# The first weight pair by eight plain products, x loaded in the order of need, and another machine model behind the instruction order

## The chip, the cores and the metric

The kernel runs on one core of a Trainium2 chip. The metric is the device time of one execution in microseconds (us); lower is better. A core has five engines that run side by side, each working through its own list of instructions in order: PE multiplies matrices, DVE (VectorE), ACT (ScalarE) and POOL (GpSimd) work element by element, and SP issues transfers between the chip's memory (HBM) and the core's own memory. POOL and ACT issue some transfers too. PE writes into eight banks of its own, each of 128 rows by 512 numbers.

## The reference

The reference is an encoder of two layers on x of 512 positions and 1024 channels. Cut to what matters:

```python
for l in range(2):
    h = rmsnorm(x, ffn1_norm[l]);  x = x + 0.5 * ((silu(h @ w_gate) * (h @ w_up)) @ w_down)
    h = rmsnorm(x, mix_norm[l]);   x = x + concat(pool, fourier, attention of h @ w_in) @ w_out
    h = rmsnorm(x, ffn2_norm[l]);  x = x + 0.5 * ((silu(h @ w_gate) * (h @ w_up)) @ w_down)
return rmsnorm(x, final_norm)
```

There are four such feed-forward blocks (1024 to 2816 and back) and two mixers. All is float32. The change touches the start of the first feed-forward block, and the order of instructions everywhere.

## The kernel before

**Layout.** x is held transposed as eight tiles `X[k]` of 128 channels by 512 positions. To keep float32 accuracy, every operand of a matmul is split into a rounded part and the remainder (`split`, L102 to L104: ACT writes `hi`, DVE writes `lo`), and one product is three matmuls: hi by hi, lo by hi, hi by lo.

**A feed-forward block.** `ffn` (L431) runs over 11 pairs of hidden row tiles in three chunks of 4, 4 and 3 pairs. After each chunk comes its part of `w_down` (tiles `dn`, 512 columns wide, L107 to L109). One pair is a `Unit` (L372). Its weights are four blocks of 512 KB, a11, a12, a21, a22: the first digit is the row tile, the second says whether they multiply the even or the odd tiles of x. The positions are halved too (`TH` = 256), so that a pair is a 2 by 2 by 2 block product. It is done with seven products in place of eight, by sums of weight blocks and sums of x blocks. One product (`product`, L378) is 24 matmuls of 256 columns, lines L386 to L388.

**Sums of weights.** A block goes by SP to one of seven staging tiles `st` (`load`, L154 to L161). A second block is added onto it in the staging tile by a transfer that POOL issues: on loading (L160, for a21 + a22) or after the tile has been split (L175, `then`). The next operand that uses the tile waits for that transfer. Splits are made three operands ahead of the one in use (`AHEAD`), into four `hi` and four `lo` tiles. `load` runs five blocks ahead (`RAWS`).

**Sums of x.** `PairNorm.scaled` (L293) multiplies each tile by its gain (tile `xg`, L296), and for each pair of tiles makes four sums of half tiles (`ta`, `tb`, L302 to L305) and four splits (`xo`, `xh`, `xl`): seven operands, by number 1 to 7.

**A unit's order.** `head` makes products 5 (sum a21 + a22) and 1 (a11); the tail of the unit before makes 4 and 3; `middle` makes 6, 7 and 2. The rms factor is applied late: `nm.end()` in the first unit's middle sums the squares across channels with two matmuls into a bank `ss` and computes the factor on DVE (L229 to L249). The squares are made by ACT (L274) and added up by POOL (L278; the last by DVE).

**The start.** SP loads the constants, then x (L194), with the first two weight blocks between. The first unit has its head `swapped`: product 1 of a11 comes first. Five matmuls on zeros (L212) run while nothing has arrived.

**What sets the order.** The code is traced in program order. On leaving the `TileContext`, the builder orders each engine's instructions: it plays the program on a model of the machine and lets each engine take the instruction that is ready in that model and stands first in the program. Buffers and banks are given out in the same pass. On the chip each engine then keeps to that list. Within the mixers the program order is the list `ORDER`, and `ON_VECTOR` and `ON_SCALAR` say which engine makes certain steps.

Of the kernel before, what the change touches and what calls it, by code (L numbers as in the profile page):

```python
# [66 lines left out]
def build(tc, xt, gu, dn, qk, wv, wfa, wo, pw, fw, small, lamv, alibi, dft_c, dft_s, out):  # L67
# [3 lines left out]
    with (  # L71
# [50 lines left out]
        for l in range(L):  # L122
            for n in range(2):
                i = 2 * l + n
                if n:
                    src = {f"P{h}": qk[l, h] for h in range(NH)}
                    src |= {"V0": wv[l, 0], "V1": wv[l, 1], "A": wfa[l, 1], "F": wfa[l, 0]}
                    src |= {"W0a": wo[l, 0], "W1a": wo[l, 1], "W2": wo[l, 2], "W3": wo[l, 3]}
                    for x in ORDER:
                        if x in src:  # L130
                            for z in range(2):
                                operand_of(raw(src[x][:, z * 1024 : (z + 1) * 1024]), eng=V if x in ON_VECTOR else G)
                for c0, c1 in CHUNKS:
                    tail = []
                    for u in range(c0, c1):
                        a11, a21, a22, a12 = [gu[i, u][:, q * 1024 : (q + 1) * 1024] for q in range(4)]
                        if raws:
                            t, t11 = raw(a21, plus=a22), raw(a11)
                        else:
                            t11, t = raw(a11), raw(a21, plus=a22)  # L140
                        t12, t22 = raw(a12), raw(a22)
                        head = [(t, a11), (t11, a21)]
                        for x, then in (head if recipes else head[::-1]) + tail + [(t, a12), (t11, None), (t12, None)]:
                            operand_of(x, then=then)
                        tail = [(t22, None), (t, None)]
                    for x, then in tail:
                        operand_of(x, then=then)
                    for m in range(KT):
                        w = 2 * (c1 - c0) * P
                        operand_of(raw(dn[i, m][:, 2 * c0 * P : 2 * c1 * P], w), w)  # L150
# [39 lines left out]
        sm = cp.tile([P, NSMALL], F32, name="sm")  # L190
        nc.sync.dma_start(sm, small)
        X = [cp.tile([P, S], F32, name=f"x{k}") for k in range(KT)]
        for k in range(KT):
            nc.sync.dma_start(X[k], xt[k])  # L194
            if k % 2:
                load(min(k // 2 + 1, 2 + (k > 6)))
        al = cp.tile([P, 896], F32, name="al")
        ident = cp.tile([P, P], F32, name="ident")
        make_identity(nc, ident)
# [58 lines left out]
        class Norm:  # L258
# [10 lines left out]
                V.tensor_scalar(self.h[k], X[k], gain, None, MUL)  # L269
                V.scalar_tensor_tensor(self.l[k], X[k], gain, f(self.h[k]), MUL, SUB)  # L270

            def squared(self, k):
                sq = g(name="sq")
                A.activation(sq, X[k], AF.Square)  # L274
                if self.acc is None:
                    self.acc = sq
                else:
                    (V if k == KT - 1 else G).tensor_tensor(self.acc, self.acc, sq, ADD)  # L278

            def end(self):  # L280
                if self.r is None:
# [4 lines left out]
        class PairNorm(Norm):  # L286
# [6 lines left out]
            def scaled(self, k):  # L293
                gain = sm[:, self.c + k : self.c + k + 1]
                self.b[k] = g(name="xg")
                A.activation(self.b[k], X[k], AF.Copy, scale=gain)  # L296
                if k % 2 == 0:
                    return
                b1, b2 = self.b.pop(k - 1), self.b.pop(k)
                c0, c1 = slice(0, TH), slice(TH, S)  # L300
                ta, tb = g(name="ta"), g(name="tb")
                V.tensor_tensor(ta[:, c0], b1[:, c0], b1[:, c1], SUB)  # L302
                V.tensor_tensor(ta[:, c1], b1[:, c1], b2[:, c1], SUB)
                V.tensor_tensor(tb[:, c0], ta[:, c1], b1[:, c0], SUB)
                V.tensor_tensor(tb[:, c1], b2[:, c0], tb[:, c0], ADD)  # L305
                one = g(F32R, name="xo")
                split(b1[:, c0], one[:, c0], one[:, c1])
                res = {1: (one[:, c0], one[:, c1])}
                for src, js in ((ta, (5, 7)), (tb, (6, 4)), (b2, (2, 3))):
# [4 lines left out]
                self.x[k // 2] = res  # L314

        class Final:

# [54 lines left out]
        class Unit:  # L372
# [2 lines left out]
            def __init__(self, nm):  # L375
                self.nm = nm

            def product(self, q, j, start, stop):  # L378
                wh, wl = operand()
                k = {"skip_group_check": True}  # L380
                for p in range(NK):
                    xh, xl = self.nm.x[p][j]
                    for z in range(2):
                        s = slice((2 * p + z) * P, (2 * p + z + 1) * P)
                        o = q[:, z * TH : (z + 1) * TH]
                        T.matmul(o, wh[:, s], xh, start=start and p == 0 and z == 0, stop=False, **k)  # L386
# [3 lines left out]
            def head(self, swapped=False):  # L390
                self.qe, self.qa = bank("qe"), bank("qa")
                for q, j in ((self.qa, 1), (self.qe, 5)) if swapped else ((self.qe, 5), (self.qa, 1)):
                    self.product(q, j, True, True)
                self.q1 = g(name="q1")
                A.activation(self.q1, self.qa, AF.Copy)

# [27 lines left out]
            def hidden(self, t):  # L424
# [3 lines left out]
                split(t[:, 0], h, lo)  # L428
                return h, lo

        def ffn(nm, nxt, first=False):  # L431
            for c0, c1 in CHUNKS:
                act, last = [], None
                for u in range(c0, c1):
                    unit = Unit(nm)
                    unit.head(first and u == 0)
                    if first and u == 0:
                        for k in range(KT):
                            nm.squared(k)
# [312 lines left out]

        nm = PairNorm(C_FFN1)
        produce(0, NK)
        pos[2] = 1
        for k in range(KT):
            nm.scaled(k)
        for l in range(L):
            nx = Norm(C_MIX + 8 * l)
            ffn(nm, nx, l == 0)  # L760
# [101 lines left out]
```

## Time and profile before

| | us |
|---|---|
| median of 3 runs | 1875.59 (1872.73 to 1879.64) |
| the profiled execution's own time | 1877.81 |
| span of its profile | 1876.0 |
| PE busy in the span | 1774.7 |
| DVE, ACT, POOL busy | 1360.3, 851.9, 320.6 |
| bytes read from HBM | 261.09 MB |

PE's busy time holds overlapping ends: a matmul of 256 columns is recorded with 0.28 us at full clock, and the next begins sooner. So progress on PE is better read from how many matmuls begin in a stretch. In the profile's rows, a name such as `lo<-st,hi` says what is written from what; behind `[` stands the idle time of the engine and what ended it. The waits name the waiting line first. "SPq" and "POOLq" are the issue queues. The granted clock of PE is given as a share of full speed.

### The profile page before, as it was taken

The page shows a single profiled execution, that of the slowest core. Times are in us where ns is not written, and L with a number is a line of the kernel's source. Part 1 is how long each engine was busy: PE and PEld are TensorE (multiplying, and loading weights), DVE is VectorE, ACT ScalarE, POOL GpSimd, SP SyncE. Part 2 cuts the span into 40 slices and gives each one's busy share as a digit, 9 for nine tenths or more (in the row PEclk, how much of TensorE's full clock was granted, in tenths as well). Part 3 has the DMA queues.
Part 4 walks back from the last instruction along what each step waited for, and adds up shares of the span by engine and source line. Part 5 has one row for each costly group of instructions (what it writes and reads, how often), then busy time and mean ns, then how long its engine had stood idle before and what let it go on. Part 6 is the DMA issues. An engine that isn't in the chain of part 4 may idle for free.

```text
span 1876.0 us, 27955 instructions
## 1 busy us (share of the span) xinstructions
PE 1774.7 (95%) x11225; PEld 1603.5 (85%) x11225; DVE 1360.3 (73%) x1956; ACT 851.9 (45%) x1189; POOL 320.6 (17%) x282
## 2 busy tenths in 40 slices
PE   5899999999879999999999999999996989999997
PEld 4898989987668999989989899898775889899896
DVE  6675765789779874855798567478987897567474
ACT  6342533448545442534555234243773554244243
POOL 3101101032322101101031010113232220010101
PEclk9899999999989999999999999999998999999998
DMA  8666867532213866857678577573322267586561
GB/s 231 150 169 137 204 165 156 138 120 85 65 42 78 188 161 147 211 151 155 161 154 195 142 167 189 129 180 124 93 71 56 65 140 197 128 193 177 127 166 45
DMA packets 76738, 265.01 MB, mean 141 GB/s; under 512 B 8640, under 2 KB 10688, under 8 KB 76608
## 3 DMA queue, kind: packets, MB, share of 16 engines
q0 software_dynamic: 25344, 92.29, 29.1%
q1 hardware_dynamic: 48096, 167.25, 27.7%
q10 hardware_dynamic: 3168, 3.68, 0.7%
q8 instruction: 88, 1.44, 0.3%
q14 instruction: 42, 0.34, 0.1%
HBM read 261.09 MB, written 2.10 MB: 140 GB/s over the span
## 4 chain that ended last, share of the span: by engine, by line
PE 69%; DVE 12%; issue 7%; DMA 5%; ACT 5%; POOL 2%; SPq 0%; DVEq 0%; ACTq 0%; POOLq 0%
PE dn L107 7%; PE dn L108 7%; PE dn L109 7%; DMA st<-in_gu 5%; PE qg L386 4%; PE qg L387 4%; PE qg L388 4%; PE qe L386 3%; PE qe L387 3%; PE qe L388 3%; PE qa L388 3%; PE qa L386 3%; PE qa L387 3%; DVE lo L104 2%; ACT hi L103 2%
## 5 line engine op out<-in xcount | busy, mean ns | idle before, releaser
L103 ACT ACTIVATE hi<-st 128x1024 fp32r<-128x1024 f32 (+2 forms) x455 | 469.2, 1036 | 668.0 <-PE dn L108 214.8
L104 DVE TENSOR_TENSOR lo<-st,hi 128x1024 fp32r<-128x1024 f32 (+2 forms) x423 | 511.5, 1213 | 179.4 <-ACT hi L103 178.3
L108 PE MATMUL dn<-al,hi 128*128 128x512 f32 x704 | 274.6, 390 | 0.0
L109 PE MATMUL dn<-ah,lo 128*128 128x512 f32 x704 | 274.1, 389 | 0.0
L107 PE MATMUL dn<-ah,hi 128*128 128x512 f32 x704 | 272.1, 392 | 0.8
L175 POOL DMA_DIRECT2D st<-in_gu x132 | 120.7, 914 | 680.3 <-DVE lo L104 606.2
L386 PE MATMUL qe<-xh,hi 128*128 128x256 f32 x704 | 203.3, 289 | 20.0 <-ACT hi L103 10.3
L386 PE MATMUL qg<-xh,hi 128*128 128x256 f32 x704 | 201.3, 286 | 8.1 <-DVE w L404 7.7
L387 PE MATMUL qe<-xh,lo 128*128 128x256 f32 x704 | 202.6, 288 | 2.2 <-DVE lo L104 2.2
L388 PE MATMUL qe<-xl,hi 128*128 128x256 f32 x704 | 202.1, 287 | 1.8 <-DVE xl L104 1.8
L387 PE MATMUL qg<-xh,lo 128*128 128x256 f32 x704 | 200.8, 285 | 2.8 <-DVE lo L104 2.8
L388 PE MATMUL qg<-xl,hi 128*128 128x256 f32 x704 | 200.6, 285 | 0.0
L452 DVE SCALAR_TENSOR_TENSOR x<-dn,x 128x512 f32<-128x512 f32 x96 | 66.1, 689 | 163.2 <-PE dn L109 163.2
L107 PEld LDWEIGHTS dn<-ah,hi 128*128 128x128 f32 x704 | 131.3, 188 | 33.1 <-ACT ah L103 7.1
L386 PEld LDWEIGHTS qe<-xh,hi 128*128 128x128 f32 x704 | 137.9, 196 | 23.9 <-ACT hi L103 16.0
L108 PEld LDWEIGHTS dn<-al,hi 128*128 128x128 f32 x704 | 132.2, 188 | 29.0 <-DVE al L104 2.4
L109 PEld LDWEIGHTS dn<-ah,lo 128*128 128x128 f32 x704 | 132.2, 188 | 26.8
L386 PEld LDWEIGHTS qg<-xh,hi 128*128 128x128 f32 x704 | 136.4, 194 | 9.4 <-DVE w L404 7.6
L387 PEld LDWEIGHTS qe<-xh,lo 128*128 128x128 f32 x704 | 137.9, 196 | 4.0 <-DVE lo L104 3.1
L388 PEld LDWEIGHTS qe<-xl,hi 128*128 128x128 f32 x704 | 138.0, 196 | 2.4 <-DVE xl L104 2.0
L387 PEld LDWEIGHTS qg<-xh,lo 128*128 128x128 f32 x704 | 136.5, 194 | 3.0 <-DVE lo L104 3.0
L388 PEld LDWEIGHTS qg<-xl,hi 128*128 128x128 f32 x704 | 136.6, 194 | 0.0
(252 smaller groups left out, 3979.1 us busy)
## 6 DMA issues: line engine op xcount, KB each, us to landing
st<-in_gu SPq DMA_DIRECT2D x176, 512.0 KB, 4.5
st<-in_gu POOLq DMA_DIRECT2D x176, 512.0 KB, 5.6
st<-in_dn SPq DMA_DIRECT2D x64, 512.0 KB, 4.3
st<-in_dn SPq DMA_DIRECT2D x32, 384.0 KB, 3.3
st<-in_qk SPq DMA_DIRECT2D x16, 512.0 KB, 3.6
st<-in_wo SPq DMA_DIRECT2D x16, 512.0 KB, 3.7
st<-in_wv SPq DMA_DIRECT2D x8, 512.0 KB, 3.9
st<-in_wfa SPq DMA_DIRECT2D x8, 512.0 KB, 3.7
```

Of the source, the lines that this page charges most:

```text
L103: A.activation(hi, src, AF.Copy)
L104: (lo_eng or V).tensor_tensor(lo, src, f(hi), SUB)
L107: T.matmul(o, lh, rh, start=start, stop=False)
L108: T.matmul(o, lh, rl, start=False, stop=False)
L109: T.matmul(o, ll, rh, start=False, stop=stop)
L175: G.dma_start(t[:, 0:w], then, accum_op=ADD)
L386: T.matmul(o, wh[:, s], xh, start=start and p == 0 and z == 0, stop=False, **k)
L387: T.matmul(o, wl[:, s], xh, start=False, stop=False, **k)
L388: T.matmul(o, wh[:, s], xl, start=False, stop=stop and p == NK - 1 and z == 1, **k)
L452: V.scalar_tensor_tensor(X[m], b, 0.5, X[m], MUL, ADD)
```

## The change

Three things are edited.

- The first pair of the first block is a `FirstUnit`: eight plain products from a11, a12, a21, a22 without sums of weights. x operands for it come from `plain` (a half tile each, gain and split in one go: ACT writes the rounded part, DVE the remainder) and are used as operands 1, 0, 2, 3. The sums of x that the later units need (operands 4 to 7) are made by `sums` and `joined` while the first products run. The squares are added on DVE. The four banks of its result are held until its `tail`, which comes behind the head of the second unit and has no products of its own.
- SP's loads at the start are ordered anew: a11, the even tiles of x as first halves and then as second halves, a12, the odd tiles of x whole, then blocks up to five.
- `TileContext` gets `schedule_with_timeline_sim=True`: the builder plays the whole program on its other model of the machine when it orders the instructions of each engine.

```diff
                         a11, a21, a22, a12 = [gu[i, u][:, q * 1024 : (q + 1) * 1024] for q in range(4)]
-                        if raws:
-                            t, t11 = raw(a21, plus=a22), raw(a11)
-                        else:
-                            t11, t = raw(a11), raw(a21, plus=a22)
+                        if not raws:
+                            for x in (a11, a12, a21, a22):
+                                operand_of(raw(x))
+                            continue
+                        t, t11 = raw(a21, plus=a22), raw(a11)
...
-        for k in range(KT):
+        load(1)
+        for c in range(2):
+            for k in range(0, KT, 2):
+                nc.sync.dma_start(X[k][:, c * TH : (c + 1) * TH], xt[k][:, c * TH : (c + 1) * TH])
+        load(2)
+        for k in range(1, KT, 2):
             nc.sync.dma_start(X[k], xt[k])
-            if k % 2:
-                load(min(k // 2 + 1, 2 + (k > 6)))
+        load(RAWS)
...
+            def plain(self, k, c):
+                gain = sm[:, self.c + k : self.c + k + 1]
+                s, c0, c1 = slice(c * TH, (c + 1) * TH), slice(0, TH), slice(TH, S)
+                o = g(F32R, name="xo")
+                A.activation(o[:, c0], X[k][:, s], AF.Copy, scale=gain)
+                V.scalar_tensor_tensor(o[:, c1], X[k][:, s], gain, f(o[:, c0]), MUL, SUB)
+                j = (1, 0)[c] if k % 2 == 0 else (2, 3)[c]
+                self.x.setdefault(k // 2, {})[j] = o[:, c0], o[:, c1]
+
+            def sums(self, p):
+                b = [g(name="xg") for _ in range(2)]
+                for z in range(2):
+                    k = 2 * p + z
+                    A.activation(b[z], X[k], AF.Copy, scale=sm[:, self.c + k : self.c + k + 1])
+                self.joined(*b, self.x[p])
...
+        class FirstUnit(Unit):
+            def head(self):
+                self.c = [[bank("qc") for _ in range(2)] for _ in range(2)]
+                for js, n in (((1, 0), True), ((2, 3), False)):
+                    w = operand()
+                    for q, j in zip(self.c[0], js):
+                        self.product(q, j, n, not n, w)
+                    if n:
+                        for p in range(NK):
+                            self.nm.sums(p)
+            def middle(self):
+                for js, n in (((1, 0), True), ((2, 3), False)):
+                    w = operand()
+                    for q, j in zip(self.c[1], js):
+                        self.product(q, j, n, not n, w)
+                for x in self.nm.x.values():
+                    del x[0]
+                for k in range(KT):
+                    self.nm.squared(k, V)
+            def tail(self):
+                self.nm.end()
+                res = []
+                for q in self.c:
+                    t = halves(wide("t"))
+                    for i in range(2):
+                        s = slice(i * TH, (i + 1) * TH)
+                        r = self.nm.r[:, s].unsqueeze(1).to_broadcast([P, 2, TH])
+                        V.tensor_tensor(t[:, :, s], halves(q[i]), r, MUL)
+                    res.append(self.hidden(t))
+                return res
...
         nm = PairNorm(C_FFN1)
         produce(0, NK)
-        pos[2] = 1
-        for k in range(KT):
-            nm.scaled(k)
+        for c in range(2):
+            for k in range(0, KT, 2):
+                nm.plain(k, c)
+        produce(1)
+        for c in range(2):
+            for k in range(1, KT, 2):
+                nm.plain(k, c)
+        pos[2] = 2
...
-    with _tile.TileContext(nc) as tc:
+    with _tile.TileContext(nc, schedule_with_timeline_sim=True) as tc:
```

`joined` is the second half of the former `scaled`: the four half sums and their splits, with the splits of operands 1, 2 and 3 left out where the caller has them already.

More of the change, by code (lines that the diff above doesn't have):

```diff
@@ L136, in build @@
                         a11, a21, a22, a12 = [gu[i, u][:, q * 1024 : (q + 1) * 1024] for q in range(4)]
-                        if raws:
-                            t, t11 = raw(a21, plus=a22), raw(a11)
-                        else:
-                            t11, t = raw(a11), raw(a21, plus=a22)
+                        if not raws:
[3 more added lines that the diff above has]
+                        t, t11 = raw(a21, plus=a22), raw(a11)
                         t12, t22 = raw(a12), raw(a22)
-                        head = [(t, a11), (t11, a21)]
-                        for x, then in (head if recipes else head[::-1]) + tail + [(t, a12), (t11, None), (t12, None)]:
+                        for x, then in [(t, a11), (t11, a21)] + tail + [(t, a12), (t11, None), (t12, None)]:
                             operand_of(x, then=then)
@@ L270, in scaled, with squared @@
                 V.scalar_tensor_tensor(self.l[k], X[k], gain, f(self.h[k]), MUL, SUB)
-            def squared(self, k):
+            def squared(self, k, eng=G):
                 sq = g(name="sq")
@@ L277, in squared @@
                 else:
-                    (V if k == KT - 1 else G).tensor_tensor(self.acc, self.acc, sq, ADD)
+                    (V if k == KT - 1 else eng).tensor_tensor(self.acc, self.acc, sq, ADD)
             def end(self):
@@ L299, in scaled, with joined @@
                 b1, b2 = self.b.pop(k - 1), self.b.pop(k)
+                self.x[k // 2] = self.joined(b1, b2)
+            def joined(self, b1, b2, res=None):
                 c0, c1 = slice(0, TH), slice(TH, S)
@@ L305, in scaled @@
                 V.tensor_tensor(tb[:, c1], b2[:, c0], tb[:, c0], ADD)
[L306 to L309, printed above, removed]
+                src = [(ta, (5, 7)), (tb, (6, 4))]
+                if res is None:
+                    one = g(F32R, name="xo")
+                    split(b1[:, c0], one[:, c0], one[:, c1])
+                    res = {1: (one[:, c0], one[:, c1])}
+                    src.append((b2, (2, 3)))
+                for src, js in src:
                     hi, lo = g(F32R, name="xh"), g(F32R, name="xl")
@@ L313, in scaled @@
                         res[j] = hi[:, c], lo[:, c]
-                self.x[k // 2] = res
+                return res
[13 more added lines that the diff above has]
+                self.joined(*b, self.x[p])
         class Final:
@@ L376, in __init__, with product @@
                 self.nm = nm
-            def product(self, q, j, start, stop):
-                wh, wl = operand()
+            def product(self, q, j, start, stop, w=None):
+                wh, wl = w or operand()
                 k = {"skip_group_check": True}
@@ L388, in product @@
                         T.matmul(o, wh[:, s], xl, start=False, stop=stop and p == NK - 1 and z == 1, **k)
-            def head(self, swapped=False):
+            def head(self):
                 self.qe, self.qa = bank("qe"), bank("qa")
-                for q, j in ((self.qa, 1), (self.qe, 5)) if swapped else ((self.qe, 5), (self.qa, 1)):
-                    self.product(q, j, True, True)
+                self.product(self.qe, 5, True, True)
+                self.product(self.qa, 1, True, True)
                 self.q1 = g(name="q1")
@@ L429, in hidden, with head @@
                 return h, lo
+        class FirstUnit(Unit):
+            def head(self):
+                self.c = [[bank("qc") for _ in range(2)] for _ in range(2)]
[25 more added lines that the diff above has]
+                    res.append(self.hidden(t))
+                return res
         def ffn(nm, nxt, first=False):
@@ L434, in ffn @@
                 for u in range(c0, c1):
-                    unit = Unit(nm)
-                    unit.head(first and u == 0)
-                    if first and u == 0:
-                        for k in range(KT):
-                            nm.squared(k)
+                    unit = FirstUnit(nm) if first and u == 0 else Unit(nm)
+                    unit.head()
                     if last:
@@ L754, in build @@
         produce(0, NK)
-        pos[2] = 1
-        for k in range(KT):
-            nm.scaled(k)
+        for c in range(2):
[6 more added lines that the diff above has]
+        pos[2] = 2
         for l in range(L):
```

## The prediction

> **What bounds the kernel now.** I first cut the span into stages and read the table of busy time by stage:
>
> ```profile
> core 0: us, PE busy (x) PEld busy (x) DVE busy (x) ACT busy (x) POOL busy (x), PEclk, DMA share, GB/s
> 0.00:100.00 100.00, 71.41 (x471) 67.19 (x472) 67.68 (x99) 47.49 (x70) 23.01 (x29) 0.91 0.76 189
> 100.00:390.00 290.00, 289.72 (x1924) 266.59 (x1924) 197.12 (x235) 114.81 (x136) 39.38 (x39) 1.00 0.65 160
> 390.00:600.00 210.00, 186.80 (x861) 151.22 (x859) 176.73 (x353) 120.72 (x220) 57.27 (x34) 0.97 0.28 75
> 600.00:700.00 100.00, 95.70 (x705) 90.83 (x705) 80.44 (x103) 47.97 (x61) 13.24 (x14) 0.97 0.69 169
> 940.00:1050.00 110.00, 105.54 (x763) 100.33 (x761) 94.33 (x121) 55.03 (x72) 19.53 (x19) 0.97 0.74 173
> 1305.00:1510.00 205.00, 184.23 (x847) 149.27 (x845) 173.58 (x346) 119.86 (x218) 55.91 (x34) 0.97 0.29 76
> 1510.00:1610.00 100.00, 93.07 (x709) 89.08 (x710) 82.41 (x109) 48.15 (x61) 13.23 (x14) 1.00 0.68 168
> ```
>
> Inside a feed-forward block PE is full (289.72 of 290 us). It is idle in four kinds of place: the first 100 us (28.6 us), the two mixers (23.2 and 20.8 us) and the starts of the other three blocks (4.3, 4.5 and 6.9 us). From 100 to 390 us PE never waits, so what is won ahead of 100 us reaches the end whole, as long as the transfers keep up; they are busy 0.65 of that stretch.
>
> How long the start should be is read from the count of matmuls. The first matmul of `w_down` begins when the four units' products are nearly through, and I take it as the mark:
>
> ```profile
> L107 PE MATMUL dn<-ah,hi x64: 388/389/499, 119.5 to 168.9; 128*128 128x512 f32 x64
> core 0: us, PE busy (x), PEclk, DMA share, GB/s
> 23.70:29.10 5.40, 5.22 (x22) 1.00 0.58 122
> 100.00:110.00 10.00, 10.00 (x84) 1.00 0.91 228
> core 0: us, PE busy (x) PEld busy (x) DVE busy (x) ACT busy (x) POOL busy (x), PEclk, DMA share, GB/s
> 0.00:30.00 30.00, 12.53 (x47) 10.15 (x48) 17.92 (x41) 15.86 (x29) 4.67 (x12) 1.00 0.88 262
> 30.00:119.36 89.36, 78.24 (x587) 76.24 (x586) 65.06 (x77) 40.98 (x52) 19.20 (x18) 0.90 0.71 165
> ```
>
> At full speed 84 matmuls begin in 10 us, 0.119 us each. Ahead of the mark there are 634, of which 5 are the matmuls on zeros and 2 those of `ss`: 627, worth 74.6 us. So 44.9 us of the 119.5 are lost. After 30 us the loss is 89.4 less 587 x 0.119, or 19.5 us; before it 25.4 us. The timeline of the start shows why:
>
> ```profile
> 0.75 0.39 SPq L191 DMA_DIRECT2D sm<-in_small  x1
> 4.02 2.42 SPq L194 DMA_DIRECT2D x<-in_xt  x4
> 8.27 0.58 PE L386 MATMUL qa<-xo,hi 128*128 128x256 f32 x1 [3.45 <-ACT hi L103]
> ...
> 22.61 1.06 ACT L103 ACTIVATE hi<-st 128x1024 fp32r<-128x1024 f32 x1 [7.21 <-DMA st<-in_gu]
> 23.57 0.40 ACT L103 ACTIVATE xo<-xg 128x256 fp32r<-128x256 f32 x1
> ...
> 23.72 0.58 PE L386 MATMUL qe<-xh,hi 128*128 128x256 f32 x1 [9.79 <-ACT hi L103]
> ```
>
> PE starts at 8.27 us, soon runs dry, and waits 9.79 us for the split of the second operand. That is the sum a21 + a22, and its added transfer, the longest piece of the chain of waits here, lands only at 22.6. Behind that split ACT's queue holds the copies of x (`xo` at 23.57) whose inputs were there long before: the order put a waiting instruction ahead of ready ones. The chain then goes on through POOL and again through added transfers:
>
> ```profile
> 2.13 5.65 DMA st<-in_gu
> ...
> 10.74 11.84 DMA st<-in_gu
> ...
> 43.80 1.57 POOL sq L278
> 45.44 2.15 POOL sq L278
> ...
> 60.20 8.42 issue
> 68.63 14.30 DMA st<-in_gu x2
> ```
>
> **The change: the first unit.** The plain products need no added transfer, so the wait of 9.79 us and its fellows go. In their place stands one more product (24 x 0.119 = 2.9 us on PE) and more work on DVE. The prices:
>
> ```profile
> L104 DVE TENSOR_TENSOR lo<-st,hi 128x1024 fp32r<-128x1024 f32 x8 | 12.3, 1555 | 10.9 <-ACT hi L103 10.9
> L104 DVE TENSOR_TENSOR xl<-ta,xh 128x512 fp32r<-128x512 f32 x4 | 2.7, 684 | 0.0
> L302 DVE TENSOR_TENSOR ta<-xg 128x256 f32<-128x256 f32 x4 | 1.7, 420 | 2.0 <-ACT xg L296 2.0
> L104 DVE TENSOR_TENSOR xo<-xg,xo 128x256 fp32r<-128x256 f32 x4 | 1.7, 418 | 0.0
> L278 DVE TENSOR_TENSOR sq<-sq,sq 128x512 f32<-128x512 f32 x1 | 0.7, 692 | 2.5 <-POOL sq L278 2.5
> L104 DVE TENSOR_TENSOR lo<-st,hi 128x256 fp32r<-128x256 f32 x4 | 1.4, 420 | 0.4 <-ACT hi L103 0.4
> L278 POOL TENSOR_TENSOR sq<-sq,sq 128x512 f32<-128x512 f32 x6 | 9.4, 1569 | 3.3 <-ACT sq L274 3.1
> st<-in_gu SPq DMA_DIRECT2D x11, 512.0 KB, 6.7
> st<-in_gu POOLq DMA_DIRECT2D x9, 512.0 KB, 5.7
> engine op xcount: duration ns min/median/max, first and last start us, forms
> L194 SPq DMA_DIRECT2D x<-in_xt x8: 421/432/744, 1.2 to 5.9; - x8
> DMA to landing us min/median/max: 2.7/6.5/7.2
> ```
>
> *PE's start.* a11 is issued second, at about 1.2 us, and x in halves behind it, 0.43 us apart. A landing takes 2.7 us for the first of x and 5.65 for the first block before; nothing is ahead of a11 now, so I take 5 and PE starts at 7.0 (between 6 and 9). Eight even halves, a12 and four odd tiles follow on SP, 13 issues x 0.43, so the last odd tile is issued at about 6.8 and lands by 14.0; it is needed at about 15. The three blocks queued behind it are needed from 21 on.
>
> *The half clock.* After its restart at 23.7, PE did 22 matmuls in 5.4 us, half the full rate, for 5.3 us. I charge the same once: 2.6 us.
>
> *PE's walk.* Four operands of 48 matmuls, 5.7 us each: from 7.0 with the half clock, the first unit ends at 7.0 + 2.6 + 22.8 = 32.4.
>
> *DVE's walk* from 6.0: first split 4 x 0.42, 16 remainders of `plain` (no such row; the nearest is the `xo` of 0.418) 6.7, a12, a21, a22 at 1.23 each 3.7, four `sums` of 4 x 0.42 + 2 x 0.684, 12.2. That is 30.3, with the first sums near 20, so operand 5 for the second unit is there in time, just. The two next splits (2.5) and the seven adds of squares (4.8) carry DVE to 37.6, the rms factor to about 44. DVE is the engine that comes short here: until `tail` has read them, the four banks of the first unit stay taken, and with `qe`, `qa`, `ss`, `qb` all eight are, so product 7 of the second unit may wait. The second unit's added transfers start after its first split, at 31.5, and land 5.7 later, 38 to 40, when product 6 wants them. The squares leave POOL, where an add took 1.569 us against 0.692. Stalls: 1.5 for product 6, 3 for a bank, and 3 to 5 for a late added transfer in the third or fourth unit, about 9 us.
>
> *The sum* to the mark: 7.0 + 2.6 + 651 x 0.119 (77.5) + 9 = 96, against 119.5: 23 us, of which I book 22. Bounds from rows: if the stretch after 30 us loses 19.5 as before, the gain is 119.5 - 7.0 - 2.6 - 77.5 - 19.5 = 13; if it loses 2, 30. `al`, the squares' ACT work and the two `ss` matmuls stay as they are.
>
> Loading x by 128 KB halves has a rule against it. The Trainium skill, "DMA: Bandwidth & Descriptors", section "Measured (HBM→SBUF, 128 partitions, SWDGE, issued from GpSimd)", gives 64 KB at 138 GB/s and 1 MB at 341. By it the even tiles would take some 2 us longer; an estimate from that page gives 20 us in place of 22. The row above has only 256 KB loads, so nothing here shows halves.
>
> **The change: the order.** No row shows the other model's order. What it can move is bounded by what order costs now: PE's 44 us of idle time in the mixers and 15.7 at the later starts. In the mixers PE waits for other engines' queues, not for data:
>
> ```profile
> PE PL L108 <- DVE g L104: 10.9, 2, 5.5
> PE PL L107 <- ACT g L103: 8.3, 4, 2.7
> PE GH L107 <- ACT g L103: 7.8, 2, 3.9
> ```
>
> A third of these 60 us, 20, is the most I expect gained. On the loss side, `ORDER`, `ON_VECTOR` and `ON_SCALAR` are fixed lists that go with the present order, so the mixers' idle time may grow by half, 22 us. I book 0, since the rows favour neither: the head-of-line case on ACT at 22.61 says that the present model misjudges transfers, the full PE from 100 to 390 that it mostly does no harm.
>
> **The rivals.**
> - *The start gains little* (13 us, 1863): the losses after 30 us repeat, since the added transfers of the later units pace them. For: the 14.30 us piece at 68.63. Against: 2 MB of added transfers of the first unit are gone and the other starts lose only 4.3 to 6.9.
> - *The order gains too* (22 + 20, 1833). For: ACT's queue at 22.61. Against: the mixers' waits are short pieces with data dependences.
> - *The order eats the gain* (22 - 22, 1875): the mixers lose half as much again.
> - *Slower*: the splits or POOL's added transfers get a later place in their queues, and each of the three other blocks starts like this one does after 30 us, losing 19.5 in place of 4 to 7 idle: 3 x 13 = 39, less 22, plus 17, or 1892. It decides from 8 us per start on.
> - *The order comes out alike*: then 1854 stands.
>
> The Trainium skill, "TensorE: Matmul & The Clock Gate", section "What's actually happening", has PE at full clock after some 3.4 us of activity. By it the half clock would cost 1.7 instead of 2.6; the traced 5.3 us is longer and is what I use.
>
> **How the numbers follow.** The profiled execution took 1877.81 with a span of 1876.0, 2.2 us (0.12%) above the median of 1875.59; the gain is taken off the median: 1875.6 - 22 = 1854. Chances: this 0.48, little gain 0.13, order gains 0.15, order eats it 0.12, slower 0.12. About 0.5% (9.4 us) is what a measurement tells from no change, so faster is below 1866, slower above 1885. Faster: all of the first but its edge, most of the second, the third, 0.72. Same: the fourth and edges, 0.15. Slower 0.13. The likeliest case alone runs from 1843 to 1866; the range, 1830 to 1882, takes in most of the others.
>
> **What would show it.** Right: PE's first product near 7 us; no added transfer ahead of the second unit; no wait over 3 us before 32; the first `w_down` matmul near 96 us; the mixers' idle time within some us of 23 and 21. Wrong: waits on `ta` or on banks near 32 to 47 us (DVE short), a dry spell near 60 to 80 (transfers), or idle time in the mixers or at the later starts that differs by over 8 us.

## The result, and the profile after

The changed kernel is slower: 1966.20 us (1964.54 to 1971.72, four runs) beside 1877.48 for the kernel before on the same chip, a ratio of 1.0481 with a 95% interval of 1.0454 to 1.0507. The profiled execution took 1971.72 with a span of 1970.0, 94.0 us over the span before.

I cut both spans at the same places: the first matmul of each block's first `dn`, the first of `pp`, the last of `wo`, and between the second and the third block the last hi-by-hi matmul of `dn`. The first two lines below are worked out from the starts of those matmuls; the others are runs told of further down.

```
us                          start  block1  mixer1 start2 block2 start3 block3  mixer2 start4 block4
before            1876.0    119.5  268.3   205.8   87.0  267.5   84.9  269.0   204.6   85.6  283.8
after             1970.0    107.2  270.4   233.0  101.7  271.5   96.0  272.9   232.2   96.7  288.4
new start alone   1863.6    105.5  267.8   205.9   87.4  267.5   84.7  269.4   205.8   86.0  283.6
order alone       1963.3    104.6  272.2   233.1   97.7  271.5   91.9  273.0   232.2   98.5  288.6
PE pinned         1888.0    120.6  268.3   207.9   88.1  267.8   87.0  269.6   205.9   89.1  283.7
others pinned     1944.5    120.8  270.2   226.6   96.6  269.6   84.0  268.6   229.9   92.8  285.4
all pinned        1872.4    117.3  268.3   205.3   86.1  267.6   84.9  268.9   201.8   88.2  284.0
```

"block" is the rest of a block behind its first `dn`, "start" what lies before it. The first start became 12.3 us shorter. The mixers lost 27.2 and 27.6, the three later starts 14.7, 11.1 and 11.1, and the four rests 2.1, 4.0, 3.9 and 4.6. All ten stages together give the 94.0.

The start in the kernel after: the `w_down` mark (as the view by tile has it), PE's timeline, the table by window, and ACT's timeline.

```profile
L107 PE MATMUL dn<-ah,hi x64: 389/389/500, 107.2 to 156.9; 128*128 128x512 f32 x64
```

```profile
7.69 0.58 PE L414 MATMUL qc<-xo,hi 128*128 128x256 f32 x1 [2.86 <-ACT xo L332]
...
46.73 0.58 PE L414 MATMUL qa<-xo,hi 128*128 128x256 f32 x1 [8.19 <-ACT q L423]
...
64.59 0.55 PE L414 MATMUL qe<-xh,hi 128*128 128x256 f32 x1 [5.59 <-DVE t L490]
```

```profile
core 0: us, PE busy (x) PEld busy (x) DVE busy (x) ACT busy (x) POOL busy (x), PEclk, DMA share, GB/s
7.70:32.50 24.80, 24.80 (x191) 24.76 (x192) 20.73 (x41) 19.59 (x34) 3.00 (x4) 1.00 0.94 316
32.50:70.00 37.50, 23.52 (x151) 22.75 (x150) 28.34 (x41) 16.10 (x23) 4.11 (x5) 0.77 0.66 141
```

```profile
40.04 1.06 ACT L103 ACTIVATE hi<-st 128x1024 fp32r<-128x1024 f32 x1 [1.67 <-DMA st<-in_gu]
41.00 4.25 ACT L278 ACTIVATE sq<-x 128x512 f32<-128x512 f32 x8
...
46.10 0.57 ACT L423 ACTIVATE q<-qa 128x512 f32<-128x512 f32 x1
```

Up to 32.5 us PE is full: 191 matmuls begin in 24.8 us, and the old wait of 9.79 us is gone. Then come two waits. The 8.19 us stand behind ACT's queue: a split that waits for an added transfer at 40.04, and eight squares ahead of the next split and of the copy `q` that PE wants. The 5.59 us are for the banks that the first unit holds until its tail (`t`, L490).

The waits of PE over the whole run (line, what it waits for: total, times, longest) show where the mixers' time went. They hold for both mixers together. Before, `GH` on `g` had 7.8 us, `ss` on `osh` 3.0 and `T` on `sc` 2.3. `PL` had 8.3 on ACT's `g` and 10.9 on DVE's (the prediction shows both rows), 19.2 in all, so that it grew by 5 alone; `ss`, `GH` and `T` grew by 11.0, 9.5 and 4.6.

```profile
PE PL L107 <- ACT g L103: 24.1, 4, 8.9
PE GH L107 <- ACT g L103: 17.3, 2, 8.7
PE ss L258 <- ACT osh L103: 14.0, 4, 6.9
...
PE T L582 <- DVE sc L574: 6.9, 2, 3.4
```

The timeline of the first mixer shows how. First PE, after; then PE, before; then DVE and ACT, after.

```profile
485.25 0.80 PE L258 MATMUL ss<-osh,ones 128*128 128x512 f32 x1 [6.87 <-ACT osh L103]
485.84 0.63 PE L107 MATMUL pp<-xh,hi 128*128 128x512 f32 x1
...
492.14 0.39 PE L259 MATMUL ss<-osl,ones 128*128 128x512 f32 x1
...
507.55 0.58 PE L107 MATMUL GH<-g,g 128*128 128x256 f32 x1 [8.67 <-ACT g L103]
...
533.61 0.79 PE L107 MATMUL PL<-g,g 128*128 128x512 f32 x1 [8.88 <-ACT g L103]
```

```profile
483.07 0.50 PE L254 MATMUL ss<-osh,ones 128*128 128x512 f32 x1 [1.52 <-ACT osh L103]
484.42 0.50 PE L255 MATMUL ss<-osl,ones 128*128 128x512 f32 x1 [0.85 <-POOL osl L104]
```

```profile
516.15 0.42 DVE L104 TENSOR_TENSOR g<-cs,g 128x256 fp32r<-128x256 f32 x1 [9.11 <-PE pp L108]
```

```profile
518.12 1.06 ACT L103 ACTIVATE hi<-st 128x1024 fp32r<-128x1024 f32 x1 [10.63 <-PE pp L108]
```

Three things are to be seen. Before this `ss` matmul (the first of a head's sum of squares) PE stands idle 6.87 us, although the twenty `pp` matmuls behind it need nothing of `osh`. Then the second `ss` matmul, which ends the sum, comes only after those twenty, at 492.14; before, the two stood next to each other in the queue. And ACT and DVE wait 9 to 11 us for a `pp` matmul: neither split reads anything from `pp`, so I read the wait as one for a buffer that the `pp` matmul still reads. With PE's order changed, the buffers come free in another order too.

### The profile page after: what moved, and what is told of

It reads as the page before. It is cut to its first block, busy times and chain, and to the rows that moved or that the text cites. A ratio compares the mean times of both kernels' runs of the same rounds, so it can differ in the third digit from the quotient of the medians.

```text
span 1970.0 us, 28009 instructions
## 1 busy us (share of the span) xinstructions
PE 1807.0 (92%) x11249; PEld 1627.0 (83%) x11249; DVE 1353.4 (69%) x1962; ACT 851.6 (43%) x1193; POOL 298.5 (15%) x272
## 4 chain that ended last, share of the span: by engine, by line
PE 65%; DVE 14%; issue 7%; ACT 7%; DMA 7%; POOL 1%; SPq 0%; ACTq 0%; DVEq 0%; POOLq 0%
PE dn L107 7%; PE dn L109 6%; PE dn L108 6%; DMA st<-in_gu 6%; PE qg L415 4%; PE qg L416 4%; PE qg L414 4%; PE qe L414 4%; PE qa L416 3%; PE qa L415 3%; PE qa L414 3%; PE qe L415 3%; PE qe L416 3%; DVE lo L104 3%; ACT hi L103 2%
## 5 line engine op out<-in xcount | busy, mean ns | idle before, releaser
L104 DVE TENSOR_TENSOR lo<-st,hi 128x1024 fp32r<-128x1024 f32 (+2 forms) x420 | 502.3, 1199 | 220.7 <-ACT hi L103 217.8
L107 PE MATMUL dn<-ah,hi 128*128 128x512 f32 x704 | 269.4, 393 | 12.1 <-ACT ah L103 7.7
L175 POOL DMA_DIRECT2D st<-in_gu x129 | 116.0, 903 | 627.0 <-DVE lo L104 606.6
L414 PE MATMUL qe<-xh,hi 128*128 128x256 f32 x608 | 174.8, 288 | 16.6 <-ACT xh L103 5.7
L416 PE MATMUL qe<-xl,hi 128*128 128x256 f32 x608 | 174.1, 286 | 0.0
L415 PE MATMUL qe<-xh,lo 128*128 128x256 f32 x608 | 174.0, 286 | 0.0
L107 PEld LDWEIGHTS dn<-ah,hi 128*128 128x128 f32 x704 | 131.7, 188 | 44.9 <-ACT ah L103 10.6
L108 PEld LDWEIGHTS dn<-al,hi 128*128 128x128 f32 x704 | 132.2, 188 | 27.6 <-DVE al L104 1.3
L414 PEld LDWEIGHTS qe<-xh,hi 128*128 128x128 f32 x608 | 118.4, 195 | 18.9 <-ACT xh L103 6.4
L414 PE MATMUL qa<-xo,hi 128*128 128x256 f32 x424 | 122.4, 289 | 10.6 <-ACT q L423 8.2
L416 PE MATMUL qa<-xo,hi 128*128 128x256 f32 x424 | 122.6, 289 | 6.3 <-DVE xo L104 6.3
```

The lines of the kernel that those rows point to most:

```text
L104: (lo_eng or V).tensor_tensor(lo, src, f(hi), SUB)
L107: T.matmul(o, lh, rh, start=start, stop=False)
L108: T.matmul(o, lh, rl, start=False, stop=False)
L175: G.dma_start(t[:, 0:w], then, accum_op=ADD)
```

## The experiments

Twelve kernels, numbered in the order in which they ran. Below, "the first model" is the one that the kernel before uses, "the other model" the one that `schedule_with_timeline_sim=True` selects. In the rows of runs 7, 8 and 10 to 12 the lines stand three or four lower: L110 there is L107 elsewhere.

**1 and 2. Each part alone.**

```diff
 run 1, the kernel after without the flag:
-    with _tile.TileContext(nc, schedule_with_timeline_sim=True) as tc:
+    with _tile.TileContext(nc) as tc:
 run 2, the kernel before with the flag:
-    with _tile.TileContext(nc) as tc:
+    with _tile.TileContext(nc, schedule_with_timeline_sim=True) as tc:
```

> The changed kernel with the builder's first model of the machine, so only the new start is left. Theory (the start gains, the order loses): the first matmul of w_down near 107 us or before, the mixers' stages (first pp to last wo) at 206 and 205 us as in the kernel before, the time about 12 us under it, 1865 (1855 to 1870). Rival (the new start upsets the rest, through buffers and banks given out differently): mixers at 233 and 232 us as in the changed kernel, the time near 1960.

> The kernel before with the builder's other model of the machine, so only the order is changed. Theory (the order loses): the mixers' stages at about 233 us each, the starts of the later blocks longer by 10 to 15 us each, the time near 1978 (1960 to 1990). Rival (the two parts interact, the order loses only together with the new start): within 10 us of 1877.

The start alone: 1864.98 us, 0.9940 of before (0.9921 to 0.9959). The order alone: 1966.94, 1.0474 (1.0441 to 1.0507). So the whole loss lies in the flag. The parts don't add up, though: by the two alone the change should cost 77 us and it cost 89. The table says why. The other model's order shortens the old start as well, to 104.6 us. The two gains, 14.0 and 14.9 us, are for the same idle time, and together they give 12.3. The start of run 1, from ACT's timeline, PE's, and the table by window:

```profile
27.51 1.06 ACT L103 ACTIVATE hi<-st 128x1024 fp32r<-128x1024 f32 x1 [4.57 <-DMA st<-in_gu]
...
41.18 0.63 ACT L103 ACTIVATE xh<-tb 128x512 fp32r<-128x512 f32 x1 [1.10 <-DVE tb L313]
```

```profile
40.13 0.58 PE L414 MATMUL qe<-xh,hi 128*128 128x256 f32 x1 [3.42 <-ACT xh L103]
...
49.10 0.58 PE L414 MATMUL qa<-xo,hi 128*128 128x256 f32 x1 [4.98 <-ACT q L423]
...
63.42 0.36 PE L414 MATMUL qe<-xh,hi 128*128 128x256 f32 x1 [1.54 <-DVE t L490]
```

```profile
32.50:70.00 37.50, 26.28 (x172) 24.73 (x170) 30.92 (x46) 20.16 (x29) 3.67 (x5) 0.77 0.60 126
```

The old fault is back one unit later: the second unit's first split (a21 + a22) stands at the head of ACT's queue until 27.51, with the sums of x behind it. They end near 42 us.

**3, 4 and 5. Which queue carries the loss.** The kernel before is built twice in one program. The first model's order of each queue is noted; then, in the build with the other model, the instructions of one queue are tied to each other in that noted order, by edges that order only and add no semaphore.

```diff
+    with _tile.TileContext(nc) as tc:
+        build(tc, **args)
+    order = {}
+    for x in nc.all_instructions():
+        order.setdefault(str(x.engine), []).append(x.name)
+    nc, args = declared()
+    with _tile.TileContext(nc, schedule_with_timeline_sim=True) as tc:
+        build(tc, **args)
+        by = {x.name: x for x in nc.cur_bb.bb.instructions}
+        for e in ('PE',):      # run 4: Activation, DVE, Pool, SP; run 5: all five
+            row = [n for n in order["EngineType." + e] if n in by]
+            for p, q in zip(row, row[1:]):
+                tc.add_manual_dep(by[q], p, edge, reason="order")
```

> The kernel before under the other model, with the queue of PE alone pinned to the order of the first model (edges from each matmul to the next, in the first model's order); the other queues follow the other model. Theory (the loss sits in the order of PE's own queue, which is in step with no engine that feeds it): the mixers' stages back to 206 us, the time within 15 us of 1877. Rival (the loss sits in the order of ACT's and DVE's queues): the mixers' stages stay near 233 us, the time near 1967.

> The kernel before under the other model, with the queues of ACT, DVE, POOL and SP pinned to the order of the first model, and PE's queue following the other model. Theory (PE's own order): the mixers' stages stay near 233 us, the time near 1967. Rival (ACT's and DVE's queues): back to 206 us per mixer and about 1877.

> The kernel before under the other model, with all five queues pinned to the order of the first model, so only the choice of buffers and banks is left to the other model. Theory (order alone makes the loss): within 4 us of 1877. Rival (buffers and banks given out differently make the loss, by new waits for their release): clearly over 1890.

PE pinned: 1891.62 us, 1.0081 (1.0053 to 1.0110). The four others pinned: 1946.07, 1.0365 (1.0343 to 1.0387). All five: 1874.25, 0.9988 (0.9974 to 1.0002). With all queues as before nothing is lost, so what buffers and banks the other model hands out costs nothing by itself. PE's order alone, put back, brings back 75 of the 89 us, the other four queues' 21. By the table, PE's order mends the mixers, the later starts (88.1, 87.0, 89.1) and the rests of the blocks; the first start goes back to 120.6, so the short start needs PE's new order too. Run 4 has it, with the other queues as before, and its start takes 120.8: the short start needs both. For the later starts the other queues count as well: with them put back, run 4 has 96.6, 84.0 and 92.8, where run 2 had 97.7, 91.9 and 98.5. The rests of the blocks can be placed: of the 16.7 us that they lose in run 2, 14.0 are waits of the `dn` matmuls for `ah`, `hi` and `lo`, which the kernel before and run 3 don't have. The later starts can be placed in part: in the three together product 1 (`qa`) waits 10.6 us for the split of its operand `xo`, where before it waited 0.9; the other waits there are short and of many kinds. From the waits of run 2 over the whole run:

```profile
PE dn L107 <- ACT ah L103: 8.6, 8, 1.2
...
PE dn L107 <- ACT hi L103: 4.6, 12, 0.5
```

The waits in run 4 still have the other order's pattern:

```profile
PE PL L107 <- ACT g L103: 23.8, 4, 7.1
...
PE ss L254 <- ACT osh L103: 12.7, 4, 6.0
PE GH L107 <- ACT g L103: 11.9, 2, 6.0
```

So PE waits for ACT here though ACT's queue stands as it did before: it is PE that asks too early and answers too late.

**6. The squares earlier.** Run 1 with each pair's squares traced right behind its sums of x, their adds on POOL as in the kernel before.

```diff
                         for p in range(NK):
                             self.nm.sums(p)
+                            self.nm.squared(2 * p)
+                            self.nm.squared(2 * p + 1)
...
-                for k in range(KT):
-                    self.nm.squared(k, V)
```

> The new start under the first model, with the squares of x traced behind the sums of x (the adds on POOL as in the kernel before) in place of behind the first unit's products. Theory (ACT's eight squares stand ahead of a split that PE needs, and the rms factor comes late): the wait of 4.98 us of product 2 of the second unit goes, and the later waits for the banks too; first matmul of w_down near 100 us in place of 105.5, the time near 1860. Rival (the waits are set by the added transfers, or POOL's adds hold DVE up as in the kernel before): 1863 to 1870.

A miss, as the rival had it: 1866.92 us, 0.9947 (0.9927 to 0.9968), with the mark at 106.9. The wait of 4.98 us did go, but the `qe` products wait 3.82 and 2.63 for `xh` in its place, and 4.18 for the banks. POOL's adds, and DVE's half sums beside them (the two timelines of run 6):

```profile
33.35 3.01 POOL L282 TENSOR_TENSOR sq<-sq,sq 128x512 f32<-128x512 f32 x2
```

```profile
33.18 2.07 DVE L310 TENSOR_TENSOR ta<-xg 128x256 f32<-128x256 f32 x1
35.17 1.48 DVE L311 TENSOR_TENSOR ta<-xg,xg 128x256 f32<-128x256 f32 x1
36.68 0.42 DVE L312 TENSOR_TENSOR tb<-ta,xg 128x256 f32<-128x256 f32 x1
```

Half sums of 0.42 us take 1.5 to 2.1 while POOL adds, and 0.42 again once it has done. So moving the adds to DVE was more than the 0.692 for 1.569 us that I counted.

**7. PE's order in the mixers alone.** As run 3, with only the PE instructions traced in the two mixers tied.

```diff
+            i0 = len(nc.cur_bb.bb.instructions)
             mixer(l, nm, nx)
+            inside.update(x.name for x in list(nc.cur_bb.bb.instructions)[i0:])
...
+        row = [n for n in order["EngineType.PE"] if n in by and n in inside]
```

> The kernel before, ordered by the other machine model, with PE's queue held to the first model's order inside the two mixers alone (from the first matmul of a mixer to its last); everything else, on PE too, stays in the other model's order. Theory (the loss is made in each stage by PE's order there): the mixers go from 233.1 and 232.2 us back to 206 to 210 each, the starts of the later blocks stay at 92 to 98, and the time is 1966.9 less about 53, that is 1908 to 1920. Rival (a stage loses by what comes to it late from other engines' queues, or by the order of the whole): a mixer keeps 220 us or more, and the time stays above 1940.

1907.69 us, 1.0172 (1.0151 to 1.0194), 0.3 us below the lower edge of what was forecast. The stages: mixers 207.6 and 207.6; the first start keeps its 106.1, the later ones stay long at 93.9, 92.7 and 94.0, the rests at 272.3, 271.5, 273.0 and 287.9. So the mixers' loss is local: with PE's order put back there alone it is gone but for 2 to 3 us each. The starts behind the mixers give back 3.8 and 4.5 us with it; the rest of their loss stays, as do the losses of the other stages.

**8, 10 and 11. What in the mixers' PE order costs.** Run 8 ties only the second `ss` matmul of each sum ahead of what follows it in the first model's order. Run 10 adds to it the v products, S and T, tied among themselves. Run 11 ties the complement: all of a mixer's matmuls but v, S and T.

```diff
 run 8:
+            second.add([x for x in nc.cur_bb.bb.instructions][-1].name)
             return b
...
+            if p in second:
+                tc.add_manual_dep(by[q], p, edge, reason="order")
 runs 10 and 11, on leaving each step n of a mixer (run 11 with "not"):
+                if n in ("V0", "V1") or n[0] in "ST" and n[1:].isdigit():
+                    inside.update(x.name for x in list(nc.cur_bb.bb.instructions)[i0:])
```

> The kernel before, ordered by the other machine model, with one kind of instruction moved on PE alone: the second matmul of each sum of squares (of an RMS norm) is tied ahead of the matmul that follows it in the first model's order, so that it is no longer up to twenty matmuls late. Theory one (the late second matmul delays the norm's factor and all that waits for it): 15 to 30 us come back, 1937 to 1952. Rival (the loss lies in the fill between the mixer's dependent steps: v products that were used up early, and half products interleaved): within 6 us of 1967.

> As the run with the second matmul of each sum of squares tied (1951.7 us), and besides the v products, score products (S) and transposes (T) of each mixer are held on PE to the first model's order among themselves, so that v products stand between S and T again; pp, GH, PL and the rest of PE stay as the other model has them. Of the mixers 222.7 and 222.5 us were left against 205.8. Theory (half of the rest or more lies in the missing fill): the wait of T on sc falls from 6.9 to under 4 us, the mixers go to 210 to 216 each, and the time is 1925 to 1939. Rival (the rest lies in the half products pp that are interleaved and hold PL and GH back): mixers 219 or more, 1944 to 1955.

> The complement inside the mixers: on PE all of a mixer's matmuls except v, S and T (that is pp, the sums of squares, GH, PL, FG, FP, AV and wo) are held to the first model's order among themselves; v, S and T stand as the other model puts them. With both parts the time was 1907.7 us and the mixers 207.6; with neither 1966.9 and 233.1. Theory of the missing fill: mixers 213 to 220, 1922 to 1940. Rival (interleaved products): the waits of PL on g fall from 24.2 to under 12 us, mixers 207 to 212, 1907 to 1920.

```
us                          mixer1   mixer2   time
order alone                 233.1    232.2    1966.94
second ss tied (8)          222.7    222.5    1951.67   1.0406 (1.0380 to 1.0432)
 + v, S, T tied (10)        221.7    221.7    1943.00   1.0347 (1.0323 to 1.0371)
all but v, S, T tied (11)   213.1    212.2    1913.13   1.0201 (1.0177 to 1.0224)
all tied (7)                207.6    207.6    1907.69   1.0172 (1.0151 to 1.0194)
```

The waits of PE, of run 8 and then of run 11:

```profile
PE PL L110 <- ACT g L106: 24.2, 4, 8.9
PE ss L257 <- ACT osh L106: 13.3, 4, 6.7
...
PE T L526 <- DVE sc L518: 6.9, 2, 3.4
...
PE GH L110 <- ACT g L106: 2.5, 2, 1.2
```

```profile
PE PL L110 <- ACT g L106: 12.8, 4, 4.5
...
PE GH L110 <- ACT g L106: 7.7, 2, 4.5
```

Of some 27 us that a mixer loses, the late second `ss` matmul makes about 10: with it in place, the wait of `GH` falls from 17.3 to 2.5 us. In time that is 15.3 us, just inside the 15 to 30 of theory one. My theory for run 10, the used-up fill of v products, fell: tied on top of run 8 it brings 1.0 and 0.8 us in the mixers. The wait of `T` on `sc` did fall below 4 as forecast, from 6.9 to 2.8, but S now waits 4.4 for `nb` and 2.1 for `kl` in its place. The span became 5.4 us shorter, most of it by other stages (the three later starts together 6.6 less, the first 2.8 more). On top of the rest (run 11 to run 7) the fill is worth 5 per mixer. Run 11 ties `pp` with `GH`, `PL`, the sums and all else but v, S and T, and this is worth 20 of the 27, including the `ss`; which of these matmuls makes the half that the `ss` doesn't was not tried apart. The mixers, at 213.1 and 212.2, came out between the ranges of theory and rival. The time fell into the rival's with help from outside: the starts behind the mixers take 89.5 and 90.9 us, 8 less than in run 2 each. `PL`'s wait came down to 12.8, not quite to the 12 that I had set, and that of `ss` on `osh` to 3.7.

**9. The second unit's split behind the sums of x.** Run 1, with that split queued behind the sums on ACT and DVE.

```diff
-                    w = operand()
+                    if n:
+                        w = operand()
+                    else:
+                        with tc.issue_after(last[0]), tc.issue_after(last[1]):
+                            w = operand()
```

> The start alone in the first model's order, and the second unit's first added weight tile, whose split stood at the head of ACT's and DVE's queues at 27.5 us, is queued behind the sums of x. Theory (that split held the queue, so the sums were done at 42.5 us and not at 30): the sums end at 31 to 36, the wait of 3.42 us ahead of the first qe product goes, the first w_down matmul starts at 100 to 103 us and not at 105.5, and the time is 1859 to 1862. Rival (the split is then late itself and product six waits as long as the others did): mark 104 to 107, time 1863 to 1868.

1863.67 us, 0.9939 (0.9921 to 0.9957). ACT's timeline, PE's, and the mark:

```profile
30.75 0.63 ACT L103 ACTIVATE xh<-tb 128x512 fp32r<-128x512 f32 x1 [0.29 <-DVE tb L313]
...
42.02 2.00 ACT L103 ACTIVATE hi<-st 128x1024 fp32r<-128x1024 f32 x2 [1.38 <-DMA st<-in_gu]
```

```profile
44.56 0.39 PE L414 MATMUL qa<-xo,hi 128*128 128x256 f32 x1 [4.87 <-ACT q L423]
...
59.60 0.55 PE L414 MATMUL qe<-xh,hi 128*128 128x256 f32 x1 [3.89 <-DVE t L496]
```

```profile
L107 PE MATMUL dn<-ah,hi x64: 389/389/500, 102.5 to 151.5; 128*128 128x512 f32 x64
```

On the start the theory held: the last sum's copy is at 30.75, the sums end near 32 us and not 42, the wait of 3.42 is gone, the mark comes 3.0 us earlier. The time did not follow: 1863.67 lies in the rival's range, and of the 3.0 us 1.5 are left in the span. The second mixer and the start behind it together became 3.4 us longer (204.8 and 90.4), the third block's rest 1.6 shorter (267.8). Why was not tried. The next wait, 4.87, is at a split that waits for a block at 42.02: there a transfer is late, and `q` with it.

**12. The old start with the other model's order.** The kernel before in the first model's order, but with all five queues tied to the other model's order from the first instruction to the first `w_down` matmul.

```diff
                 act += last.tail()
+                if first and c0 == 0:
+                    first_start.update(x.name for x in nc.cur_bb.bb.instructions)
...
+            row = [n for n in order["EngineType." + e] if n in first_start]
```

> The kernel before, ordered by the first model as it was, but all five queues of its first chunk up to the first w_down matmul are held to the order that the other model gave them, in which that start took 104.6 us and not 119.5 with the same products. Theory (a start's time is set by the order in it alone): first w_down matmul at 104 to 107 us, the rest of the kernel as before, 1859 to 1866, as fast as the new products. Rival (the short start came with what the other order does further on, as a shift of work out of it): the mark moves but the time stays within 4 us of 1875.

1863.73 us, 0.9931 (0.9912 to 0.9949). The mark, ACT's queue and PE:

```profile
L110 PE MATMUL dn<-ah,hi x64: 389/389/506, 104.5 to 155.3; 128*128 128x512 f32 x64
```

```profile
20.60 1.04 ACT L106 ACTIVATE hi<-st 128x1024 fp32r<-128x1024 f32 x1
```

```profile
21.70 0.58 PE L389 MATMUL qe<-xh,hi 128*128 128x256 f32 x1 [0.72 <-ACT hi L106]
```

With the old products and the old loads, the split of a21 + a22 now stands behind the copies of x, at 20.60, and PE's wait of 9.79 us is 0.72. But that is not yet where the time is won: `qe` begins only 2.0 us earlier (21.70 for 23.72). The tables by window, of run 12 and then of before:

```profile
0.00:40.00 40.00, 24.93 (x110) 20.75 (x111) 28.14 (x50) 27.35 (x46) 14.98 (x20) 0.96 0.85 249
40.00:60.00 20.00, 20.00 (x167) 19.91 (x166) 18.22 (x24) 7.93 (x10) 3.45 (x4) 1.00 0.97 223
```

```profile
0.00:40.00 40.00, 20.67 (x110) 17.89 (x111) 25.75 (x50) 25.01 (x44) 8.14 (x16) 1.00 0.85 241
40.00:60.00 20.00, 15.07 (x86) 13.99 (x85) 12.82 (x13) 5.43 (x7) 9.45 (x8) 0.74 0.66 148
```

By 40 us both have begun 110 matmuls. In the 20 us behind that it is 167 against 86: run 12 has ACT's squares since 26.8 and PE does not wait, while before the squares end at 40.4, PE waits for splits and at 50.39 for the sum of squares, and its granted clock is 0.74. Which of the five queues makes this was not tried apart. The time equals that of runs 1 and 9 within their intervals. These three, 1863.67 to 1864.98 us, are the fastest kernels of the study, and run 6 lies within their intervals too; run 12 gets there with the old products and loads, by order alone. The profiled execution of run 12 was the fastest of its six (1856.21), so its span of 1854.4 is not set beside the others.

## Why the prediction was wrong, step by step

Forecast were 1854 us, and faster. The step that failed is the order, booked at 0 between 20 us won and 22 lost: alone it costs 89.5 us (run 2). In its place the runs showed a queue of PE that asks for operands before they are there and puts ready matmuls behind: put back, PE's order returns 75 of these us (run 3), and in the mixers alone 59 (run 7).

- *PE's start at 7.0*: 7.69 after, 7.5 in run 1. Right. The Trainium skill, "DMA: Bandwidth & Descriptors", section "Measured (HBM→SBUF, 128 partitions, SWDGE, issued from GpSimd)", has small transfers slow, which by the prediction's estimate from it would have made the even tiles some 2 us late. Here PE is busy from 7.70 to 32.50 without a gap, so it cost nothing; these loads go by SP, and the Trainium skill's figures there are for transfers issued from GpSimd.
- *The half clock, 2.6, and the first unit's end at 32.4*: 191 matmuls in 24.8 us are 2.1 more than 191 x 0.119, and the last `qc` began at 32.5 after, 32.2 in run 1. Right. The PEclk of 1.00 in that row, as in the prediction's row from 23.70, does not show the half rate, since the trace's first clock record is at 11.7 us after and at 29.1 before. The spacing does: 0.21 us up to 11.6, 0.12 from 11.8 on.
- *DVE's walk, sums of x done at 30.3*: right as a sum of work (32.1 in run 9), wrong as a queue. In run 1 they ended near 42 us, since the split of a21 + a22 stood ahead of them at 27.51. I had named just that fault as the one of the kernel before, and then let the new sequence run as if nothing could stand in it.
- *Stalls of 9 us*: a size. In run 1, 172 matmuls began from 32.5 to 70 us; at 0.119 each that leaves 17.0 us lost. Of these PE was idle 11.2 (its busy time there is 26.28), and 5.8 went into slow matmuls behind each new wait. I had booked the half clock once. The bank stall was forecast at 3 and measured 5.59 after, 1.54 in run 1; the late added transfer, forecast for the third or fourth unit, came in the second.
- *The mark at 96, a gain of 22*: 105.5 in run 1, a gain of 14.0 there and 12.5 us in the time. This is the rival "the start gains little" (13, 1863): what is lost after 30 us repeats. The reason given there, added transfers, is a part of it (the split at 27.51); the longest wait, of 4.98, stands behind the eight squares and the copy `q` in ACT's queue, and run 6, which moved the squares, was no faster.
- *The order at 0*: the step that failed, with three errors in one. The mixers' loss was bounded at half of their idle time, 22 us for both, and measured 54.9. The blocks' inner parts were held safe since PE is full there, and they lost 16.7. And "the rows favour neither" was wrong as an argument: rows of the present order can bound what a better order gains, namely the idle time that is left, but nothing in them bounds what a worse one loses. For the later starts, the rival "slower" had 39 us together, and run 2 lost 30.6 there: 10.7, 7.0 and 12.9. But its mechanism, splits and added transfers with a later place in other queues, is at most half of it: PE's own order, put back, leaves 6.7 of the 30.6 (run 3), the other queues put back leave 15.9 (run 4). And that the mixers' waits are "for other engines' queues, not for data" is not in the rows shown for it, which name the split `g` as what is waited for; further down the prediction says itself that they have data dependences.
- *The profile of the order as evidence*: I took the head-of-line wait at 22.61 as a sign that the other model could gain at the start. It did: 14.9 us on the old start (run 12 keeps 11.9 of them in the time). The sign was right and the place was partly luck: by 40 us run 12 is no further than before, and wins behind that.

What is settled: the loss is order and not buffers (run 5), mostly PE's (run 3), in the mixers made within them (run 7), and there by the late halves of sums (10 of 27 us) and by the places of the other matmuls but v, S and T (10 more), little by the missing fill (runs 8, 10, 11). That interleaved `pp` products make the second 10 is argued, not shown. Seen in the waits, but not tried apart: what costs the 7 to 13 us of the later starts and the 4 us of each block's rest. Why the other model prefers such an order was not looked into.

## What to carry to other kernels

An edit that reorders every queue is a change to the whole kernel, however small its diff: price it by stage, and leave the losing side open by as much as a queue's dependent pairs can be pulled apart, not by the idle time that stands now. In a profile, look for an instruction that waits while ready ones stand behind it, and for the two halves of one sum standing apart; both can be mended by tying single pairs in place, and a good order for one stage can be kept there alone. Before work is added to win idle time, try whether an order alone wins it.

## What was not expected of the hardware

Waiting costs PE more than the wait. The first mixer of run 2 and of the kernel before, the same 843 matmuls in each:

```profile
376.80:610.00 233.20, 194.69 (x843) 156.41 (x842) 166.08 (x341) 114.49 (x208) 49.02 (x30) 0.90 0.23 64
```

```profile
387.80:593.60 205.80, 184.88 (x843) 149.18 (x842) 172.49 (x348) 119.46 (x218) 56.54 (x34) 0.97 0.28 76
```

The mixer grew by 27.4 us. PE's idle time grew from 20.9 to 38.5, which is 17.6; the other 9.8 are longer busy time of the same matmuls, at a mean granted clock of 0.90 where it was 0.97. After the wait of 6.87 us shown above, `pp` matmuls begin 0.43 us apart up to 489.25 and 0.23 apart from 489.6 on; the granted clock is 0.50 from 482.8 to 489.4 and 1.00 from 489.6 to 503.

And POOL's adds stretched DVE's half sums by a factor of 3.5 to 5 in run 6 (0.42 to 1.48 and 2.07 us). What they share was not measured apart.
